# A decoder layer on one core: the order of its first 40 microseconds rebuilt

## The chip, the cores and the metric

The kernel runs on one core of one Trainium2 chip. The core has five engines that run beside each other, each with its own queue, taken strictly in order: TensorE (PE; its weight loads are listed as PEld), VectorE (DVE), ScalarE (ACT), GpSimd (POOL) and SyncE (SP), which here only issues DMA transfers. Engines wait for each other by semaphores. The metric is the device time of one execution in microseconds (us); lower is better.

## The reference

One layer of a decoder trunk over 256 positions of width 2048, all in fp32:

```python
mod = silu(c) @ w_ada + b_ada                      # 6 segments of 2048
shift1, scale1, gate1, shift2, scale2, gate2 = split(mod, 6)
h = rms_norm(x, norm1_gain) * (1 + scale1) + shift1
x = x + gate1 * mixing_sublayer(h, w_in, ...)      # h @ w_in, three attention branches, output projection
h = rms_norm(x, norm2_gain) * (1 + scale2) + shift2
x = x + gate2 * swiglu(h, w_ffn_in, w_ffn_out)
```

with `rms_norm(x, g) = x * rsqrt(mean(x*x) + eps) * g`. For the beginning only the first three lines matter: nothing of `h @ w_in` can start before the norm of x, and before shift1 and scale1, each of which is a product of silu(c) with a 2048 x 2048 part of `w_ada`. Later parts (attention, gated linear attention, branch gates, output projection, feed-forward) are the same before and after.

## The kernel before, in words

**Products in three matmuls.** A product keeps fp32 accuracy by splitting both operands: `hi` is the value rounded to the matmul's format (fp32r), `lo` what is left. `mm3` (L151 to L154) adds hi x hi, hi x lo and lo x hi into one PSUM bank. A weight piece is loaded by SP into one of four `raw` buffers (L135), cast to `whi` on ScalarE (L146) and subtracted to `wlo` on VectorE (L147); then `raw` is free again.

**Blocks and groups.** `h @ w_in` is computed in column blocks of 512 (13 blocks, `proj_block`), for both halves of the 256 positions. The 16 tiles of 128 along the width are taken in four groups, `GROUPS` = 0 to 3, 3 to 7, 7 to 11, 11 to 16. A group's 13 blocks need only that group's h, so the first blocks can start when shift1 and scale1 are known for three tiles. A block of the first group has 3 tiles x 2 halves x 3 matmuls = 18 matmuls. Results go to `A[b]` by copies on ScalarE (L415).

**Shift and scale.** `ada_group` computes them without TensorE's big products: SP loads a piece of `w_ada` for each of 16 tiles k (L269; for the first group 128 x 768: three tiles of shift and of scale), and VectorE multiplies it by silu(c) of that tile and adds it to `acc` (`ada_mac`, L247 and L249). At the end `column_sum` (L292) sums over the partitions by a matmul with ones; `finish_columns` (L298, L301) adds b_ada and applies norm1_gain. The next group's pieces are loaded and added while a group's blocks run.

**The norm of x.** `norm1` loads x in four pieces of 128 x 1024 (L344), sums squares on ScalarE (L355), combines them on VectorE (L356, L358), and takes 1/sqrt by `rsqrt`: Ln and Exp on ScalarE (L232, L233) and one Newton step on VectorE (L230, L235 to L238). ScalarE scales x in place (L362), TensorE turns it in 32 transposes (L366), ScalarE copies the result to `xT` (L367). `make_h` (L376 to L378) makes h from it: hi and an fp32 copy on ScalarE, lo on VectorE.

**Vectors.** `load_vectors` brings gains and biases as rows (three loads on SP, L207 to L209, seven on POOL, L216 to L219) and turns them into columns with two transposes (L221, L224). c has its own load and transpose (L190, L192) and becomes `csil` = silu(c).

**What sets the order.** A planner orders each engine's queue ahead of time: among instructions that its own estimate of time holds ready, it takes the one of highest priority. `prio` raises the priority of what is written inside it; otherwise what is written earlier goes first. `tc.issue_after(i)` puts the instructions inside it behind instruction i, when they are on i's engine. Tiles named by a tag (`S(tag, ...)`) share one place in memory; a new tile of the tag waits until the old one is read for the last time. `scr` is a pool of three such places. In the old beginning, four pieces of `w_ada` are issued (`XAT`), then the norm and the vectors, then the other pieces; the junk output of the squares, c, and the two tiles of vector rows all take `scr` places.

Of the kernel before, what the change touches and what calls it, by code (L numbers as in the profile page):

```python
# [34 lines left out]
XAT = 4  # L35
AHEAD = 4000
FIN = 13
# [28 lines left out]
def trunk(ctx: ExitStack, tc: tile.TileContext, I, out):  # L66
# [57 lines left out]
    def load_weights(src, k0, k1, c0, w=NB, spare=()):  # L124

        parts = []
        step = (2 * NB) // w  # L130
        with prio():
            for ka in range(k0, k1, step):
                n = min(step, k1 - ka)
                raw = wp.tile([P, step, w], F32, tag="raw", name=nm("raw"))
                nc.sync.dma_start(  # L135
                    raw[:, :n, :],
                    src[ka * P : (ka + n) * P, c0 : c0 + w].rearrange("(k p) c -> p k c", p=P),
                )
# [7 lines left out]
                nc.scalar.copy(hi[:, :n, :], raw[:, :n, :])  # L146
                state["split"] = nc.vector.tensor_tensor(lo[:, :n, :], raw[:, :n, :], hi[:, :n, :].bitcast(F32), op=ALU.subtract)  # L147
                parts += [(hi[:, i, :], lo[:, i, :]) for i in range(n)]
        return parts
# [27 lines left out]
    make_identity(nc, ident)  # L177
    ones = const.tile([P, P], F32, name="ones")
    nc.vector.memset(ones, 1.0)
    ones_r = const.tile([P, P], F32R, name="ones_r")  # L180
    nc.scalar.copy(ones_r, ones)
# [10 lines left out]
    nc.tensor.transpose(c_ps, crow[:KC, :], ident[:KC, :KC])  # L192
# [8 lines left out]
    rows = scr([P, P])  # L201
    brow = scr([P, P])
# [3 lines left out]
    def load_vectors():  # L206
# [3 lines left out]
        for r, name in (  # L210
            (ROW_SBQ, "sb_q_gain"),
            (ROW_SBK, "sb_k_gain"),
            (ROW_DILQ, "dil_q_gain"),
            (ROW_DILK, "dil_k_gain"),
        ):
            nc.gpsimd.dma_start(rows[r : r + 1, :], I[name])  # L216
        nc.gpsimd.dma_start(rows[ROW_GB : ROW_GB + 4, :], by_chunk("b_gla_a"))
        nc.gpsimd.dma_start(rows[ROW_GG : ROW_GG + 2, :], by_chunk("gla_out_gain"))
        nc.gpsimd.dma_start(rows[0:16, :], by_chunk("c"))  # L219
# [4 lines left out]
        nc.tensor.transpose(bada_ps, brow[:96, :], ident[:96, :96])  # L224
# [66 lines left out]
    def column_sum(ps, acc):  # L291
        nc.tensor.matmul(ps, acc, ones[:, 0:1], start=True, stop=True)  # L292
# [47 lines left out]
    def norm1():  # L340
        xin = [S(f"A{9 + j}", [P, 2, NB]) for j in range(4)]
        for t in range(NT):
            for hf in range(2):
# [3 lines left out]
                )  # L347
        for t in range(NT):
            ss2 = small([P, 2])
            for hf in range(2):  # L350
                junk = scr([P, 512])
                xs = xin[2 * t + hf]
                pa = small([P, 2])
                for q in range(2):
                    nc.scalar.activation(junk, xs[:, q, :], AF.Square, accum_out=pa[:, q : q + 1])  # L355
                nc.vector.tensor_add(ss2[:, hf : hf + 1], pa[:, 0:1], pa[:, 1:2])  # L356
            ss = small([P, 1])
            nc.vector.tensor_add(ss, ss2[:, 0:1], ss2[:, 1:2])  # L358
            rstd = rsqrt(ss, 1.0 / D, [P, 1])
            for hf in range(2):  # L360
                xs = xin[2 * t + hf]
                nc.scalar.activation(xs, xs, AF.Copy, scale=rstd)  # L362
                for q in range(2):
                    ps = misc_bank([P, 4, P])
                    for i in range(4):
                        nc.tensor.transpose(ps[:, i, :], xs[:, q, i * P : (i + 1) * P], ident)  # L366
                    nc.scalar.copy(xT[2 * hf + q][:, :, t * P : (t + 1) * P], ps)  # L367
# [3 lines left out]
    def make_h(k, sh, sc):  # L371
# [4 lines left out]
        nc.scalar.activation(hi, src, AF.Identity, bias=sh, scale=sc)  # L376
        nc.scalar.activation(hf, src, AF.Identity, bias=sh, scale=sc)
# [43 lines left out]
    def h_group(g):  # L421
        k0, k1 = GROUPS[g]
        sh, sc = gains[g]
        for k in range(k0, k1):
            make_h(k, sh[:, k - k0 : k - k0 + 1], sc[:, k - k0 : k - k0 + 1])

    with prio(30000):
        early = []
        g0 = ada_group(
            *GROUPS[0],  # L430
            tags=tuple(f"A{j}" for j in range(9)) + ADA_TAGS,
            between=lambda: early.extend(load_weights(w_in, *GROUPS[0], orders[0][0] * NB)),
        )
        for _ in range(XAT):
            next(g0)
        with prio():
            norm1()
            load_vectors()
        for _ in g0:
            pass  # L440
        with prio():
            h_group(0)
    qg_sb = const.tile([P, 2], F32, name="qgains")
# [4 lines left out]
    for g in range(len(GROUPS) - 1):  # L448
# [636 lines left out]
```

## Time and profile before

| | |
|---|---|
| median of 3 executions | 1640.3 us (1639.02 to 1644.5) |
| the profiled execution | 1639.62 us, of which the span is 1637.8 us |
| TensorE busy | 1599.9 us (98%), 7309 matmuls |
| VectorE, ScalarE busy | 1120.5 us, 801.8 us |
| first matmul of the first block | 34.63 us after the start of the span |
| first matmul of the second block | 40.66 us |

The span runs from the first to the last instruction of the profiled execution; times within it are counted from its start. A row of the order of time gives start, length, engine, line, operation, what is written from what, a count of merged instructions, and in brackets how long the engine was idle before and what ended that. The length of matmuls is modelled and overlaps; the distance of their starts is what they cost. The row PEclk is the share of TensorE's full clock that was granted. A plain fp32 matmul stands as two records, a transpose as one.

### The profile page before, as it was taken

How to read it: one execution, taken by the hardware profiler on the slowest of the kernel's cores; microseconds unless marked ns; L12 is line 12 of the kernel's file. 1: busy time of each engine (PE TensorE's matmuls, PEld its weight loads, DVE VectorE, ACT ScalarE, POOL GpSimd, SP SyncE). 2: the span in 40 equal slices, each digit the busy share in tenths (PEclk: the TensorE clock that was granted, in tenths of full speed). 3: DMA queues.
4: the chain of work that ended last, by engine and by line, in shares of the span. 5: the costliest groups of instructions: out<-in, count | busy, mean ns of one | idle time of the engine just before them, and what ended most of it. 6: DMA issues, size and time to landing. Idle time of an engine off the chain costs nothing.

```text
span 1637.8 us, 19950 instructions
## 1 busy us (share of the span) xinstructions
PE 1599.9 (98%) x7309; PEld 1320.3 (81%) x7309; DVE 1120.5 (68%) x1351; ACT 801.8 (49%) x1133; POOL 6.0 (0%) x14
## 2 busy tenths in 40 slices
PE   4999999999999999999999999999999999999998
PEld 3788888788778888888887888888888888888887
DVE  6789996879687687877756566766655555454453
ACT  5654448765765444444445644444444444433332
POOL 1000000000000000000000000000000000000000
PEclk9999999999999999999999999999999999999999
DMA  9999987776777899888757478888766666666663
GB/s 316 322 327 323 325 285 216 250 242 186 225 229 263 295 312 310 305 270 311 260 184 226 131 231 260 280 260 255 222 189 192 181 192 189 187 207 195 206 206 109
DMA packets 194562, 395.91 MB, mean 242 GB/s; under 512 B 12899, under 2 KB 27913, under 8 KB 194465
## 3 DMA queue, kind: packets, MB, share of 16 engines
q1 hardware_dynamic: 194240, 394.63, 74.7%
q8 instruction: 57, 0.93, 0.2%
q14 instruction: 41, 0.33, 0.1%
q0 software_dynamic: 224, 0.01, 0.0%
HBM read 392.50 MB, written 2.10 MB: 241 GB/s over the span
## 4 chain that ended last, share of the span: by engine, by line
PE 91%; DVE 3%; DMA 2%; ACT 2%; issue 1%; SPq 0%; DVEq 0%; ACTq 0%
PE acc L153 28%; PE acc L154 28%; PE acc L152 28%; DVE wlo L147 1%; DMA raw<-w_br_gla 1%; PE misc L606 1%; PE misc L871 1%; PE misc L292 1%; ACT whi L146 1%; DVE ada L249 1%; PE misc L366 0%; DMA A<-x 0%; PE misc L500 0%; DMA AR<-w_ada 0%; DMA raw<-w_ffn_in 0%
## 5 line engine op out<-in xcount | busy, mean ns | idle before, releaser
L147 DVE TENSOR_TENSOR wlo<-raw,whi 128x1024 fp32r<-128x1024 f32 (+1 forms) x548 | 653.4, 1198 | 435.9 <-ACT whi L146 432.6
L146 ACT CAST whi<-raw 128x1024 fp32r<-128x1024 f32 (+1 forms) x548 | 564.2, 1032 | 706.1 <-PE acc L154 556.5
L153 PE MATMUL acc<-wlo,H 128*128 128x512 f32 x1576 | 617.5, 392 | 3.1 <-DVE wlo L147 3.0
L152 PE MATMUL acc<-whi,H 128*128 128x512 f32 x1576 | 615.6, 392 | 2.2 <-ACT whi L146 2.1
L154 PE MATMUL acc<-whi,H 128*128 128x512 f32 x1576 | 616.0, 391 | 0.0
L153 PEld LDWEIGHTS acc<-wlo,H 128*128 128x128 f32 x1576 | 296.3, 188 | 67.0 <-DVE wlo L147 7.8
L152 PEld LDWEIGHTS acc<-whi,H 128*128 128x128 f32 x1576 | 296.0, 188 | 63.4 <-ACT whi L146 3.0
L154 PEld LDWEIGHTS acc<-whi,H 128*128 128x128 f32 x1576 | 296.3, 188 | 62.2 <-DVE H L378 0.9
L152 PE MATMUL acc<-whi,A 128*128 128x512 f32 x312 | 122.3, 392 | 0.0
L153 PE MATMUL acc<-wlo,A 128*128 128x512 f32 x312 | 121.5, 390 | 0.7 <-DVE wlo L147 0.7
L154 PE MATMUL acc<-whi,A 128*128 128x512 f32 x280 | 109.1, 390 | 0.0
L249 DVE SCALAR_TENSOR_TENSOR ada<-AR,csil,ada 128x1024 f32<-128x1024 f32 x59 | 75.1, 1278 | 1.6 <-DMA AR<-w_ada 1.5
L153 PEld LDWEIGHTS acc<-wlo,A 128*128 128x128 f32 x312 | 58.6, 188 | 13.0 <-DVE wlo L147 1.1
L152 PEld LDWEIGHTS acc<-whi,A 128*128 128x128 f32 x312 | 58.6, 188 | 12.0
L154 PEld LDWEIGHTS acc<-whi,A 128*128 128x128 f32 x280 | 52.5, 188 | 11.1
L152 PE MATMUL acc<-whi,T 128*128 128x512 f32 x120 | 46.8, 390 | 0.0
L154 PE MATMUL acc<-whi,T 128*128 128x512 f32 x120 | 46.7, 389 | 0.0
L153 PE MATMUL acc<-wlo,T 128*128 128x512 f32 x120 | 46.7, 389 | 0.0
L154 PE MATMUL acc<-whi,OS 128*128 128x512 f32 x112 | 43.6, 389 | 0.0
L415 ACT COPY A<-acc 128x512 f32<-128x512 f32 x50 | 28.6, 586 | 21.1 <-PE acc L154 20.1
L249 DVE SCALAR_TENSOR_TENSOR ada<-OS,csil,ada 128x1024 f32<-128x1024 f32 (+2 forms) x33 | 35.5, 1075 | 0.5 <-DMA OS<-w_ada 0.2
L417 DVE TENSOR_TENSOR A<-A,acc 128x512 f32<-128x512 f32 x48 | 31.9, 684 | 5.1 <-PE acc L154 4.9
(315 smaller groups left out, 1217.3 us busy)
## 6 DMA issues: line engine op xcount, KB each, us to landing
raw<-w_in SPq DMA_DIRECT2D x205, 512.0 KB, 4.7
raw<-w_ffn_in SPq DMA_DIRECT2D x176, 512.0 KB, 4.1
raw<-w_ffn_out SPq DMA_DIRECT2D x88, 512.0 KB, 4.8
AR<-w_ada SPq DMA_DIRECT2D x79, 512.0 KB, 4.9
raw<-w_out SPq DMA_DIRECT2D x32, 512.0 KB, 4.3
KC<-w_ada SPq DMA_DIRECT2D x30, 512.0 KB, 5.0
KD<-w_ada SPq DMA_DIRECT2D x19, 512.0 KB, 5.8
OS<-w_ada SPq DMA_DIRECT2D x16, 512.0 KB, 6.6
```

The costliest lines, as they stand in the source:

```text
L146: nc.scalar.copy(hi[:, :n, :], raw[:, :n, :])
L147: state["split"] = nc.vector.tensor_tensor(lo[:, :n, :], raw[:, :n, :], hi[:, :n, :].bitcast(F32), op=ALU.subtract)
L152: nc.tensor.matmul(ps, lh, rh, start=start, stop=False, skip_group_check=seeded)
L153: nc.tensor.matmul(ps, lh, rl, start=False, stop=False, skip_group_check=seeded)
L154: state["mm"] = nc.tensor.matmul(ps, ll, rh, start=False, stop=stop, skip_group_check=seeded)
L249: nc.vector.scalar_tensor_tensor(acc, raw, c, acc, op0=ALU.mult, op1=ALU.add)
L292: nc.tensor.matmul(ps, acc, ones[:, 0:1], start=True, stop=True)
L415: nc.scalar.copy(A[b][:, t, :], pss[t])
L417: nc.vector.tensor_add(A[b][:, t, :], A[b][:, t, :], pss[t])
L606: nc.tensor.matmul(ps[:, h, :], at(lhs, h, t), at(rhs, h, t), start=True, stop=True)
L871: nc.tensor.transpose(ps[:, i, :], src[:, i * P : (i + 1) * P], ident)
```

## The change

The order of the beginning is new. SP issues c, the vectors, x, and then all 16 pieces of the first group's `w_ada`, followed by the first block's `w_in`. c, the vector rows, the squares' junk, the diagonal and an operand for unused matmuls get places that belong to h later (H2, H3, H5 to H7, H0 and H1), none in `scr`. POOL's loads are put right behind the making of the identity matrix.

The norm's sums, the Newton step and the reciprocal root run on ScalarE alone, for both halves of the positions together. x is not scaled any more: TensorE multiplies each 128 x 128 tile of x by a diagonal matrix of the reciprocal roots, which turns and scales it at once. So 32 transposes become 32 plain fp32 matmuls.

Between the steps TensorE gets matmuls whose result nobody reads (`keep_warm`, 128 x 512, fp32r): 22 behind the transpose of c, 20 behind the transposes of the vectors, 32 behind the turning of x, 5 behind the column sums. The turning of the vectors is put behind the first 22, and the column sums behind the 32. The six column sums of the first group go to one PSUM tile, and all of them are issued before the first is finished.

The first block's casts on ScalarE are put behind the last copy to `xT`, and h of the first group behind these casts. The casts of later weights, up to the sixth block, are put behind the first instruction of h. In the first group the fp32 copy of h is made on VectorE. `ones_r` is made on VectorE instead of ScalarE.

```diff
-XAT = 4
+WARM = (22, 20, 32, 5)
@@ load_weights(..., ahead=True)
-                nc.scalar.copy(hi[:, :n, :], raw[:, :n, :])
+                with tc.issue_after(state["casts_after"]) if "casts_after" in state else nullcontext():
+                    state["cast"] = nc.scalar.copy(hi[:, :n, :], raw[:, :n, :])
@@
-    crow = scr([P, P])
+    crow = S("H7", [P, P])
-    rows = scr([P, P])
-    brow = scr([P, P])
+    rows = S("H6", [P, P])
+    brow = S("H5", [P, P])
@@ load_vectors: the seven POOL loads
+        with tc.issue_after(made):
...
+    def turn_vectors():
...
@@ norm1
+        for t in range(NT):
             for hf in range(2):
-                junk = scr([P, 512])
...
+                junk = S(f"H{t}", [P, 2, NB])
+                act(junk, xin[2 * t + hf], AF.Square, accum_out=part[:, hf, t : t + 1])
+        v, y, z, r = (small([P, NT]) for _ in range(4))
+        col = lambda a, t: a[:, t : t + 1]
+        for t in range(NT):
+            act(col(v, t), part[:, 0, t : t + 1], AF.Identity, bias=part[:, 1, t : t + 1])
+        act(v, v, AF.Identity, bias=eps_c[:, 0:1], scale=1.0 / D)
+        act(y, v, AF.Ln)
+        act(y, y, AF.Exp, scale=-0.5)
+        act(z, y, AF.Square)
+        for t in range(NT):
+            act(col(z, t), col(z, t), AF.Copy, scale=col(v, t))
+        act(z, z, AF.Identity, bias=eps_c[:, 1:2], scale=-0.5)
+        diag = S("H3", [P, NT, P])
+        for t in range(NT):
+            act(col(r, t), col(y, t), AF.Copy, scale=col(z, t))
+            act(diag[:, t, :], ident, AF.Copy, scale=col(r, t))
+        for j in range(4):
+            for t in range(NT):
+                ps = misc_bank([P, 4, P])
+                for i in range(4):
+                    xs = xin[2 * t + j // 2][:, j % 2, i * P : (i + 1) * P]
+                    state["turn"] = nc.tensor.matmul(ps[:, i, :], xs, diag[:, t, :], start=True, stop=True)
+                state["turned"] = nc.scalar.copy(xT[j][:, :, t * P : (t + 1) * P], ps)
+
+    def keep_warm(n):
+        ps = acc_bank()
+        for _ in range(n):
+            state["warm"] = nc.tensor.matmul(ps, ones_r, wide, start=True, stop=True)
+
+    wide = S("H2", [P, NB], F32R)
@@ make_h(k, sh, sc, early=False)
-        nc.scalar.activation(hf, src, AF.Identity, bias=sh, scale=sc)
+        if early:
+            nc.vector.tensor_scalar(hf, src, sc, sh, op0=ALU.mult, op1=ALU.add)
+        else:
+            nc.scalar.activation(hf, src, AF.Identity, bias=sh, scale=sc)
@@
+    def first_group():
...
+            nc.sync.dma_start(r, w_ada[k * P : (k + 1) * P, : 2 * D].rearrange("p (s c) -> p s c", s=2)[:, :, :w])
+            raws.append(r)
+        with tc.issue_after(state["turned"].ins):
+            early.extend(load_weights(w_in, *GROUPS[0], orders[0][0] * NB, ahead=False))
+        last_cast = state["cast"]
+        acc = S("ada", [P, 2, w])
+        for k in range(KC):
+            ada_mac(acc, raws[k], k)
+        ps = misc_bank([P, 2 * n])
+        for q in range(n):
+            for j in range(2):
+                with tc.issue_after(state["warm"].ins):
+                    last_sum = column_sum(ps[:, 2 * q + j : 2 * q + j + 1], acc[:, j, q * P : (q + 1) * P])
+        with tc.issue_after(last_sum.ins):
+            keep_warm(WARM[3])
...
     with prio(30000):
...
+        load_vectors()
+        load_x()
+        with tc.issue_after(c_turn.ins):
+            keep_warm(WARM[0])
+        with tc.issue_after(state["warm"].ins):
+            turn_vectors()
+        with tc.issue_after(state["row_turn"].ins):
+            keep_warm(WARM[1])
+        norm1()
+        with tc.issue_after(state["turn"].ins):
+            keep_warm(WARM[2])
+        last_cast = first_group()
+        with prio(), tc.issue_after(last_cast.ins):
             h_group(0)
+        state["casts_after"] = state["h_first"].ins
@@ the loop over blocks
+            if (g, n) == (0, 6):
+                state.pop("casts_after", None)
```

More of the change, by code (lines that the diff above doesn't have):

```diff
@@ L357, in norm1 @@
[L357 to L367, printed above, removed]
+                junk = S(f"H{t}", [P, 2, NB])
@@ L424, in h_group @@
         for k in range(k0, k1):
-            make_h(k, sh[:, k - k0 : k - k0 + 1], sc[:, k - k0 : k - k0 + 1])
-    with prio(30000):
[L428 to L441, printed above, removed]
+            make_h(k, sh[:, k - k0 : k - k0 + 1], sc[:, k - k0 : k - k0 + 1], g == 0)
```

71 lines of the change are left out of this document (45 added, 26 removed).

## The prediction

> **What bounds the kernel now.** I read the page first, then a table of stages, then the instructions in order of time.
>
> ```profile
> span 1637.8 us, 19950 instructions
> PE 1599.9 (98%) x7309; PEld 1320.3 (81%) x7309; DVE 1120.5 (68%) x1351; ACT 801.8 (49%) x1133; POOL 6.0 (0%) x14
> ...
> PE   4999999999999999999999999999999999999998
> ...
> PEclk9999999999999999999999999999999999999999
> DMA  9999987776777899888757478888766666666663
> ```
>
> TensorE is the bound: 37.9 us of the span are not PE, and nearly all of them lie in the first slice (41 us). A change of the beginning can win what lies there and little more. The table of stages cuts that slice and the steady part behind it:
>
> ```profile
> 16.10:20.00 3.90, 3.68 (x16) 3.28 (x16) 3.28 (x5) 3.83 (x10) 0.93 (x2) 1.00 0.78 235
> 20.00:24.10 4.10, 0.00 (x0) 0.00 (x0) 3.26 (x10) 2.65 (x7) 0.00 (x0) 1.00 0.96 305
> 24.10:27.70 3.60, 3.53 (x16) 3.28 (x16) 3.28 (x4) 2.81 (x5) 0.00 (x0) 1.00 1.05 381
> 27.70:31.10 3.40, 0.73 (x5) 0.46 (x4) 2.75 (x5) 0.84 (x3) 0.00 (x0) 1.00 1.05 388
> 31.10:34.60 3.50, 2.38 (x12) 2.29 (x12) 0.97 (x9) 1.55 (x3) 0.00 (x0) 0.50 1.05 387
> 34.60:37.90 3.30, 3.23 (x7) 1.88 (x8) 3.29 (x6) 3.30 (x7) 0.00 (x0) 0.50 0.73 209
> 54.00:87.00 33.00, 32.47 (x143) 26.58 (x143) 26.74 (x26) 20.62 (x31) 0.00 (x0) 1.00 0.94 333
> ```
>
> Each row: the stage, its length, busy time of PE, PEld, DVE, ACT and POOL, then granted clock, DMA share and GB/s. The clock is half from 31.1 to 37.9, just when the sums and the first block run. Before 27.7 the column says 1.00 only because no change was recorded yet: the transposes there (L366) take 421 ns, those at full clock later (L500) 273 ns, so it was half. DMA falls to 235 GB/s in 16.1 to 20.0. The order of time shows the path:
>
> ```profile
> 10.30 0.63 ACT L355 ACTIVATE scr<-A 128x512 f32<-128x512 f32 x1 [7.43 <-DMA A<-x]
> ...
> 29.78 1.02 DVE L249 SCALAR_TENSOR_TENSOR ada<-A,csil,ada 128x768 f32<-128x768 f32 x1
> ...
> 30.95 2.53 PE L292 MATMUL misc<-ones,ada 128*128 128x1 f32 x12 [2.67 <-DVE ada L249]
> 31.88 0.22 DVE L298 TENSOR_TENSOR mod<-misc,bada 128x1 f32<-128x1 f32 x2 [1.07 <-PE misc L292]
> ...
> 33.05 0.60 ACT L376 ACTIVATE H<-T,mod 128x256 fp32r<-128x256 f32 x1 [4.33 <-DVE mod L301]
> 33.55 1.55 ACT L146 CAST whi<-raw 128x1024 fp32r<-128x1024 f32 x2
> ...
> 34.63 1.22 PE L152 MATMUL acc<-whi,H 128*128 128x512 f32 x2 [1.16 <-ACT whi L146]
> ```
>
> The first block waits for h; h for the column sums; those for the last of 16 multiply-adds (macs) on VectorE. The second block's first matmul starts at 40.66. A block has 18 matmuls, each 0.227 us after the one before at full clock (starts 42.70, 42.93, 43.16), that is 4.09 us; so the first block cost as if it had run undisturbed from 36.57. That is the figure to beat. Last, what SP waits for in the first 100 us:
>
> ```profile
> SPq L135 <- DVE wlo L147: 41.9, 21, 5.2
> SPq L135 <- DMA raw<-w_in: 5.0, 4, 1.9
> ```
>
> Weight loads wait for a free raw buffer, not for DMA. Bandwidth is no bound once blocks run.
>
> **Vectors and x first.** SP issues c, three vectors (0.33, 0.33, 0.42 us) and four pieces of x (0.60 each) before the 16 pieces of w_ada (0.47 each): x begins at about 2.2 instead of 3.18, w_ada at 4.6 instead of 1.19. POOL's seven issues (0.5 each, 3.6 together) ran from 13.45, after a 12.1 us wait for a shared scratch buffer; they now follow the identity matrix at 1.3 and, at 4.1 to 5.5 us to landing, are there by 9.5. SP's waits for the same buffers (1.6 and 4.2 us), where DMA dipped, go. The same 2.1 + 6.3 MB come as one stream: between 351 GB/s (stage 2.4 to 16.1) and 388, from about 3.4, the last w_ada lands between 25.0 and 27.4, and its mac (1.02) ends at about 27.5, at most 28.5. The two w_in pieces (0.79 MB, 2 us) land at about 28.5.
>
> **The norm on ScalarE.** VectorE loses 16 tiny operations (about 0.155 each, 2.5 us) and their waits, so the macs (1.02 against one piece per 1.0 to 1.1 us of DMA) keep pace with the stream. ScalarE loses four scalings of x (1.14 each) and has 4 squares of 1024 columns instead of 8 of 512 (0.75 each with the read of the sum): about 1.2 each. The last x lands at about 9.7, the last square ends at 10.9. Then 13 small operations in a row, 0.24 apart (Ln to Exp, 13.75 to 13.99); those with a per-partition operand cost more: L376 with two takes 586 ns for 256 columns, the plain copy L415 takes 586 for 512, so 0.1 us each. Eleven operations with eight operands, 3.5 us: first diagonal at 14.4, second at 15.0. VectorE gains the fill of the unused matmuls' operand (between 0.17, the memset at L179, and 0.68, a 512-column subtract) and three copies of h (between 0.2, a quarter of L247's 0.745, and 0.42, L378); both lie where it is idle.
>
> **Transposes become matmuls by a diagonal.** A plain fp32 matmul stands as two records (L520: 12 for 6 heads), 0.113 apart at full clock (L606: 16 in 1.8 us). So 32 cost 64 x 0.113 = 7.2 us where 32 old transposes at half clock cost 7.36. At half clock they would cost 14.7. ScalarE's eight copies (0.59 against 0.9 per group) stay hidden.
>
> **The unused matmuls set the beat.** All are written into TensorE's order, so the start of the first block is now a sum on one queue: c turned at 2.65; 22 matmuls, 0.43 apart at half clock (L152 x2: 1.22 less the 0.79 of one). The records change at 27.7, 31.1 and 37.9, on a grid of 3.4 us; work from 24.17 had full clock after 3.5, from 34.63 after 3.3, and 3.7 us of work from 16.19 never (the next transposes still take 421 ns). So full clock comes 3.4 to 6.8 us after the start, I take 5.1: 12 slow, 10 fast, end 10.05 (9.25 to 10.85). The Trainium skill, "TensorE: Matmul & The Clock Gate", Part 1, puts the release at about 4 us into sustained work, with 0.5 either way; by it the 22 would end at 9.5 and the total be 1634.6 (an estimate). Two of the three stretches agree with it, the third does not.
>
> Vectors turned, 0.5: 10.55. 20 matmuls, 4.54: 15.1 (diagonals are there by then, with no slack for the second). Turns 7.2: 22.3. 32 matmuls, 7.26: 29.6; the macs are done, and the column sums, placed behind these matmuls, start here. Sums 12 x 0.106 (1.68 for 16 at 87.07) = 1.27, half of the 2.53 of before: 30.9. All six sums now share one PSUM tile, so I let the finishing wait for the last: three operations and h end at about 32.0. Five matmuls, 1.14: 32.0. Handover 0.1: the first block starts at **32.1** and ends at 36.2. Behind the waits stand, in order, all that TensorE does later; nothing else of it is late.
>
> **Casts.** The first block's casts (1.03 + 0.61) now run ahead of h, in ScalarE's idle time; with splits (1.22 + 0.68) they are done at about 31.0. So its matmuls need not wait as they did at 34.63, 35.89 and 36.91. Later casts stand behind the first h at 31.5; block 1's is needed at 36.2 and takes 1.7: hidden, unless h slips by over 3 us.
>
> **Sum.** 40.66 - 36.2 = 4.4 us earlier, at unchanged work behind. The profiled execution took 1639.62 (span 1637.8 and 1.8 around it), 0.7 under the median 1640.3: 1635.2. From the median that is 0.31%, and 0.3%, about what a measurement of this kernel can tell, is 1635.4. Bounds of the unknown terms: the clock's phase 0.8 either way, handovers and stalls in block 0 from 0 to 1.5: 1634.2 to 1637.5.
>
> **Rivals.**
> *A later stall goes too.* At 52.45 to 53.98 TensorE waits through a cast and its split, because on ScalarE the cast stands behind a copy of a finished block. Other order of casts could dissolve it: 1.4 less, 1633.8. Against: blocks after the seventh are ordered as ever.
>
> *The head start is eaten.* Transfers from 54 to 87 run at 333 GB/s of the 388 seen; if blocks that begin 4.4 us sooner meet the same landing times, TensorE idles as much more: 1639.6. Against: SP's 41.9 us of waits are for buffers, which come free sooner too.
>
> *The chain of the norm outlasts its cover.* No slack at 15.1: each us that x or an operand is late is a us lost; at 1.5 us, 1636.7. Over 3.4 us the clock falls too, as in 27.7 to 31.1.
>
> *The first block's splits stand ahead of macs on VectorE* (slower). The early load is now written before the macs and at the same priority, and VectorE takes its queue in order. If the planner thinks w_in lands before the last w_ada, n macs follow splits that end at 31.0: the sums start at 31.1 + 1.03 n instead of 29.6. With n = 5 (the macs not yet landed when xT is ready, 22.9) that is 36.2, +6.6: 1641.8. From n = 3 it is slower than before, from n = 9 (1646.0) by over 0.3%. For it: nothing orders splits behind macs. Against: in this trace L147 first runs at 34.61, behind all macs.
>
> **Chances.** Forecast 0.49 (0.27 under 1635.4, 0.22 over); later stall 0.18, faster; eaten 0.07 and chain 0.04, both within; splits 0.22 (0.06 within, 0.16 slower). Faster 0.45, within 0.39, slower 0.16. The range runs to 1632.8 below (stall gone and full clock early) and 1643.5 above (splits with n up to 6); about 0.2 lies outside, most of it above. The forecast's own range is 1633.5 to 1637.5.
>
> **What would show it.** First block's L152 at 31.3 to 33 and the second block's 4.1 us later; clock full from before 10 us on; no gap between the macs; L147 behind the last mac; sums at the end of the unused matmuls, not waiting for VectorE. Wrong if TensorE waits for the diagonal or for a mac, if L147 precedes an L249 of the first group, or if idle time of PE between 40 and 200 grows by over 1 us.

## The result, and the profile after

The changed kernel takes 1637.31 us in the median of 20 runs (1635.15 to 1639.23), the kernel before 1642.25 us in 20 runs beside it. The ratio is 0.9969, with a 95% interval of 0.9962 to 0.9976: 4.9 us or 0.31% faster. The profiled execution took 1638.33 us (span 1636.6).

The first view of the changed kernel is the page: the span, the busy times, and the busy share of DMA in 40 slices (41 us each).

```profile
span 1636.6 us, 20156 instructions
...
PE 1617.2 (99%) x7420; PEld 1333.7 (81%) x7420; DVE 1120.2 (68%) x1342; ACT 798.2 (49%) x1126; POOL 5.9 (0%) x14
...
DMA  9999986876778889888756478887766666666663
```

TensorE is busy for 17.3 us more, but the 79 unused matmuls alone take 21.8 us of the first slice, so the busy share says nothing about the gain. DMA is as busy as before. The span fell by 1.2 us only, less than the runs: the profiled execution of the kernel before took less time than most of its executions (1639.62; the mean of all 95 executions of it is 1642.2). We come back to this.

The order of time of the changed kernel shows how the beginning runs now (start, length, engine, line, operation; in brackets the idle time and what ended it).

```profile
10.40 1.06 ACT L366 ACTIVATE H<-A 128x1024 f32<-128x1024 f32 x1 [2.40 <-DMA A<-x]
...
12.50 1.04 ACT L366 ACTIVATE H<-A 128x1024 f32<-128x1024 f32 x1
...
16.98 7.41 PE L389 MATMUL misc<-H,A 128*128 128x128 f32 x64 [1.16 <-ACT H L383]
...
24.14 7.70 PE L396 MATMUL acc<-H,ones_r 128*128 128x512 f32 x32
...
29.56 1.02 DVE L258 SCALAR_TENSOR_TENSOR ada<-A,csil,ada 128x768 f32<-128x768 f32 x1
30.83 1.57 ACT L147 CAST whi<-raw 128x1024 fp32r<-128x1024 f32 x2 [5.82 <-DMA raw<-w_in]
...
31.68 1.39 PE L301 MATMUL misc<-ones,ada 128*128 128x1 f32 x12
31.91 1.83 DVE L148 TENSOR_TENSOR wlo<-raw,whi 128x1024 fp32r<-128x1024 f32 x2 [1.32 <-ACT whi L147]
...
33.65 0.35 DVE L307 TENSOR_TENSOR mod<-misc,bada 128x1 f32<-128x1 f32 x4
...
34.16 1.09 ACT L408 ACTIVATE H<-T,mod 128x256 fp32r<-128x256 f32 x2 [1.77 <-DVE mod L307]
...
34.81 0.50 PE L153 MATMUL acc<-whi,H 128*128 128x512 f32 x1 [0.48 <-ACT H L408]
```

Three things are to be seen. The first block starts at 34.81, no sooner than before (34.63). What precedes it is no longer TensorE's own order: the last multiply-add ends at 30.58, `w_in` is cast from 30.83, the splits follow on VectorE until about 33.7, and only then the modulation is finished (L307), so that h and the block can begin. And the first block, once started, meets no stall: the second block's first matmul runs at 39.03, that is 4.22 us later, where the kernel before needed 6.03 (34.63 to 40.66). So the start brought nothing and the block itself 1.8 us.

The table of stages says why. It cuts the changed kernel where its own work changes: stage, length, busy time of PE, PEld, DVE, ACT and POOL, granted clock, DMA share, GB/s.

```profile
0.00:10.50 10.50, 7.96 (x23) 6.05 (x23) 1.46 (x8) 2.71 (x5) 4.26 (x13) 1.00 0.66 207
10.50:16.90 6.40, 5.20 (x23) 3.89 (x22) 3.04 (x6) 6.17 (x21) 0.00 (x0) 1.00 1.06 381
...
24.10:31.70 7.60, 7.60 (x36) 6.16 (x35) 6.03 (x6) 1.48 (x3) 0.00 (x0) 1.00 1.05 380
31.70:34.80 3.10, 2.64 (x18) 2.08 (x16) 2.89 (x12) 1.33 (x4) 0.00 (x0) 1.00 1.05 387
34.80:39.00 4.20, 4.18 (x18) 3.43 (x19) 4.10 (x10) 2.52 (x4) 0.00 (x0) 1.00 0.97 359
```

The clock is full in the stages of the sums and the first block, where it was half before. DMA runs without a dip from 10.5 to 34.8 (373 to 387 GB/s). But the first 10.5 us move 207 GB/s only. In steps of 5 us, the same table of the kernel before begins with 156 and 329 GB/s and dips to 266 later; the changed kernel's begins with 59 and 337:

```profile
0.00:5.00 5.00, 0.26 (x1) 0.18 (x1) 0.76 (x4) 1.77 (x3) 0.70 (x6) 1.00 0.54 156
5.00:10.00 5.00, 0.00 (x0) 0.00 (x0) 2.66 (x3) 0.00 (x0) 0.00 (x0) 1.00 1.03 329
...
15.00:20.00 5.00, 3.68 (x16) 3.28 (x16) 4.15 (x5) 4.93 (x10) 2.03 (x5) 1.00 0.84 266
```

```profile
0.00:5.00 5.00, 2.46 (x6) 2.00 (x7) 1.46 (x8) 1.47 (x2) 4.26 (x13) 1.00 0.28 59
5.00:10.00 5.00, 5.00 (x17) 3.94 (x16) 0.00 (x0) 1.15 (x2) 0.00 (x0) 1.00 1.00 337
...
15.00:20.00 5.00, 3.84 (x31) 3.36 (x30) 4.28 (x7) 3.33 (x13) 0.00 (x0) 1.00 1.06 372
```

Summed over the six steps up to 30 us, the kernel before moves 9.27 MB and the changed one 9.53 MB: 0.26 MB more, 0.7 us of transfer at 386 GB/s. The last piece of `w_ada` gets nothing of this. In the trace it lands at 29.46, and in the kernel before at 29.26. The transfers run side by side: when that piece lands, 0.79 MB of pieces issued behind it are already there, 0.48 MB in the kernel before. The last multiply-add nevertheless ends 0.2 us sooner than before (30.58 against 30.80), because VectorE is no longer behind: it begins 0.1 us after the landing (29.56) instead of 0.5 us (29.78).

For the rest of the kernel we follow one number, the **lead**: by how much the same ScalarE and VectorE instructions run sooner than in the first profile of the kernel before (median over a stretch). In the changed kernel it is 1.4 us at 48 us and 2.4 to 2.8 from 60 to 300 us. So a further 1.0 to 1.4 us comes in between. PE's idle time from 40 to 200 us falls from 2.01 to 0.88 us. The place is the hand-over from the fourth block to the fifth. First the kernel before, then the changed one, in the order of time:

```profile
52.42 0.59 ACT L415 COPY A<-acc 128x512 f32<-128x512 f32 x1 [2.81 <-PE acc L154]
52.90 1.05 ACT L146 CAST whi<-raw 128x1024 fp32r<-128x1024 f32 x1
...
54.00 0.73 PE L152 MATMUL acc<-whi,H 128*128 128x512 f32 x2 [0.94 <-ACT whi L146]
...
55.27 0.50 PE L153 MATMUL acc<-wlo,H 128*128 128x512 f32 x1 [0.53 <-DVE wlo L147]
```

```profile
50.09 1.05 ACT L147 CAST whi<-raw 128x1024 fp32r<-128x1024 f32 x1 [1.87 <-DMA raw<-w_in]
51.05 1.25 ACT L451 COPY A<-acc 128x512 f32<-128x512 f32 x2
...
52.46 0.50 PE L154 MATMUL acc<-wlo,H 128*128 128x512 f32 x1 [0.33 <-DVE wlo L148]
```

Before, ScalarE's queue has a copy of the fourth block's result ahead of the fifth block's cast. ScalarE waits 2.81 us for that block to end, although the fifth block's weights have landed by 51.56, and TensorE then waits 0.94 and 0.53. In the changed kernel the cast stands ahead of both copies, and 0.33 us of waiting is left. Nothing in the diff names this order: the planner chose it anew. Why it did is not shown.

### The profile page after: what moved, and what is told of

It is laid out like the page before. It is cut to its first block, busy times and chain, and to the rows that moved or that the text cites. A ratio compares the mean times of both kernels' runs of the same rounds, so it can differ in the third digit from the quotient of the medians.

```text
span 1636.6 us, 20156 instructions
## 1 busy us (share of the span) xinstructions
PE 1617.2 (99%) x7420; PEld 1333.7 (81%) x7420; DVE 1120.2 (68%) x1342; ACT 798.2 (49%) x1126; POOL 5.9 (0%) x14
## 4 chain that ended last, share of the span: by engine, by line
PE 90%; DMA 4%; DVE 3%; ACT 2%; issue 1%; SPq 0%; DVEq 0%; ACTq 0%
PE acc L154 28%; PE acc L155 28%; PE acc L153 28%; DMA raw<-w_in 2%; DVE wlo L148 1%; DMA A<-w_ada 1%; PE misc L678 1%; ACT whi L147 1%; PE misc L943 1%; PE misc L301 1%; DVE ada L258 1%; DMA raw<-w_br_gla 0%; PE misc L572 0%; DMA AR<-w_ada 0%; DMA raw<-w_ffn_in 0%
## 5 line engine op out<-in xcount | busy, mean ns | idle before, releaser
L148 DVE TENSOR_TENSOR wlo<-raw,whi 128x1024 fp32r<-128x1024 f32 (+1 forms) x548 | 653.6, 1197 | 436.4 <-ACT whi L147 432.9
```

## The experiments

All kernels here compute the full result. The order of the table is that of the text; the lead is in us, and a kernel's time is the median of its runs.

```
kernel                 lead at 48   at 84   at 700   at the end   time      ratio [95% interval]
changed                  1.39       2.43    1.09       1.28       1637.31   0.9969 [0.9962, 0.9976]
a1 changed, again        1.51       3.04   -0.20       0.42       1637.55   0.9975 [0.9966, 0.9983]
a2 no unused matmuls     0.54       0.54    1.93       2.51       1639.54   0.9987 [0.9978, 0.9995]
a3 26 instead of 32      1.62       3.24    1.15       1.53       1637.35   0.9969 [0.9957, 0.9980]
a4 unused alone          0.57       0.58   -0.25       0.39       1639.85   0.9987 [0.9978, 0.9995]
b1 before, again        -0.89      -0.88   -2.29      -1.85       1641.46   (one run)
b2 x, then vectors       1.98       3.35    2.46       2.88       1637.30   0.9974 [0.9964, 0.9983]
b3 finish first          1.87       1.87    3.28       3.74       1637.74   0.9978 [0.9968, 0.9988]
b4 b2 and b3             2.53       2.56    1.27       1.77       1636.74   0.9967 [0.9954, 0.9980]
c1 before, cast first   -2.83      -1.08   -1.32      -1.20       1640.84   0.9991 [0.9981, 1.0000]
c3 changed, copy first   1.41       1.41    0.44       0.53       1638.31   0.9977 [0.9968, 0.9986]
c2 b4, cast first        2.48       3.74    1.86       2.47       1636.00   0.9967 [0.9954, 0.9979]
d1 c2, again             2.31       4.35    4.19       4.41       1636.89   0.9962 [0.9948, 0.9976]
```

**a1: the changed kernel once more.** No edit.

> The changed kernel once more, unaltered, for a second profile. In the first pair of profiles the second block's first matmul came at 39.03 instead of 40.66, 1.6 us sooner, and by 60 us the lead was 2.8; after that the lead fell by 2.0 at about 335 us and by 0.9 at about 688 us (TensorE waited for late weights) and grew by 1.7 at 488 us, where only the old kernel's clock fell to half for 3.4 us. Theory A (what comes after 60 us is chance of the single execution): second block again at 39.0 (38.6 to 39.6), and the two losses not at the same places. Theory B (the change causes the later losses): idle time of TensorE again at about 330 and 688. Time in both: ratio to before 0.996 to 0.998.

First block at 34.69, first copy of its result at 38.88, last multiply-add at 30.44: within 0.2 us of the first profile. The lead at 84 us is 3.04. Up to there the two executions agree. Then a1 loses 1.1 us between 88 and 100 us, where its clock is half from 87.23 to 90.64; the first profile has the full clock there. The table of stages of a1 has this row:

```profile
87.30:90.60 3.30, 3.23 (x8) 2.56 (x9) 2.13 (x5) 3.30 (x7) 0.00 (x0) 0.50 0.65 187
```

By 700 us a1 has lost 3.2 us, the first profile 1.3. The two waits that the theories ask about come at the same matmuls in both profiles, but differ in length: 2.88 us at 334.22 in the first, 1.13 at 333.68 in a1, and 0.71 and 1.18 near 687 us. The kernel before waits at these matmuls too (0.90 and 0.54). So the places are fixed, as theory B has it, but the change did not make them, and how long the wait is falls by execution.

**a2: no unused matmuls.** Nothing else is edited, but the planner orders VectorE and ScalarE otherwise here: the finishing of the sums goes ahead of the splits, and the fifth block's cast behind a copy again, as in the kernel before.

```diff
-WARM = (22, 20, 32, 5)
+WARM = (0, 0, 0, 0)
 def keep_warm(n):
+    if n == 0:
+        state.setdefault("warm", c_turn)
+        return
```

> All four groups of unused matmuls left out, everything else of the change kept. Theory clock: the matmuls that turn x start at half clock and warm it up, then TensorE idles from about 27 until the last multiply-add ends at 30.6, so the clock falls again in most executions; sums and first block run at half clock; second block at 40.5 to 42, 1.5 to 3 us slower than the changed kernel. Rival loads: the start is set by the transfers, the casts and VectorE, and the clock costs nothing there; second block at 39 to 39.5, time within 0.5 us of the changed kernel.

The order of time of this kernel, and then its row of stages for the first block:

```profile
31.54 0.35 DVE L307 TENSOR_TENSOR mod<-misc,bada 128x1 f32<-128x1 f32 x4 [1.72 <-PE misc L301]
...
32.71 1.22 PE L153 MATMUL acc<-whi,H 128*128 128x512 f32 x2 [1.28 <-ACT H L411]
...
33.42 1.22 DVE L148 TENSOR_TENSOR wlo<-raw,whi 128x1024 fp32r<-128x1024 f32 x1
...
34.70 0.79 PE L154 MATMUL acc<-wlo,H 128*128 128x512 f32 x1 [0.78 <-DVE wlo L148]
```

```profile
31.20:37.90 6.70, 4.65 (x13) 3.21 (x13) 6.26 (x19) 2.72 (x5) 0.00 (x0) 0.52 0.94 323
```

The first block starts 2.1 us sooner than in the changed kernel, because here the finishing (L307) stands ahead of the splits (L148). Yet its result is copied at 39.63, 0.6 us later than the changed kernel's: the clock is half (0.52) and the matmuls wait for the splits. The ratio 0.9987 is about half of the changed kernel's gain or less. The second block's first matmul comes at 40.12, between what the two theories expected. The time is 2.0 us over the changed kernel's, but not all of that is the clock, since the cast behind the copy costs 1.0 to 1.6 us of it (c3 below).

**a3: 26 instead of 32 unused matmuls behind the turns.**

```diff
-WARM = (22, 20, 32, 5)
+WARM = (22, 20, 26, 5)
```

> 26 instead of 32 unused matmuls before the column sums, all queues else in the same order. The sums could start 1.36 us sooner, at 30.7 when the last multiply-add ends. Theory VectorE: the finishing of the sums stands behind the two splits of the first weights (31.91 to 33.74), so h and the first block stay at 34.2 and 34.8: no gain, at most 0.2. Rival TensorE's written order: the first block comes at 33.4, the time falls by 1.4.

```profile
30.49 1.47 PE L301 MATMUL misc<-ones,ada 128*128 128x1 f32 x12
...
31.63 1.83 DVE L148 TENSOR_TENSOR wlo<-raw,whi 128x1024 fp32r<-128x1024 f32 x2 [1.29 <-ACT whi L147]
...
33.38 0.35 DVE L307 TENSOR_TENSOR mod<-misc,bada 128x1 f32<-128x1 f32 x4
...
34.54 0.50 PE L153 MATMUL acc<-whi,H 128*128 128x512 f32 x1 [1.31 <-ACT H L408]
```

The column sums start 1.2 us sooner (30.49 against 31.68), the first block only 0.27, and the time is the same. So the number of unused matmuls does not set the start. The splits stand between the sums and their finishing on VectorE, and they wait for casts that wait for `w_in`.

**a4: the unused matmuls alone, in the kernel before.** 18 behind the first transposes of x, 16 behind the turned vectors, 5 behind the column sums; nothing else is changed.

```diff
+WARM = (18, 16, 5)
...
+            if t == 0:
+                with tc.issue_after(state["turn"].ins):
+                    keep_warm(WARM[0])
...
+            with tc.issue_after(state["row_turn"].ins):
+                keep_warm(WARM[1])
...
+                    if k0 == 0 and q == m - 1:
+                        with tc.issue_after(last_sum.ins):
+                            keep_warm(WARM[2])
```

> The kernel before with nothing but unused matmuls added: 18 after the first 16 transposes, 16 after the transposes of the vectors, 5 after the column sums. Theory clock: sums take 1.3 instead of 2.5 and the first block runs at full clock, second block at 39.2 to 39.8 instead of 40.66, and the time falls by 1 to 2.5 us, most of what the whole change wins at the start. Rival order of loads: the last multiply-add ends at 30.8 as before and the casts still stand behind h, so the second block stays at 40.3 to 40.7 and the time within 0.5.

The row of stages shows the clock full where it was 0.50:

```profile
31.20:37.90 6.70, 5.55 (x27) 3.77 (x27) 4.50 (x16) 4.93 (x9) 0.00 (x0) 1.00 1.00 354
```

The first block starts at 34.56 and its result is copied at 39.58 instead of 40.18, though the last multiply-add ended 0.6 us later here (31.38 against 30.80). The ratio is 0.9987. The second block's first matmul comes at 40.06, again between the two theories. The clock without the new order gives as much as the new order without the clock, 0.13% each; the two together give 0.25 to 0.31%, in which the later stall (below) has a part that neither a2 nor a4 has.

**b1: the kernel before once more.** No edit.

> The kernel before once more, unaltered, for a second profile of it. Theory phase: the clock changes on a grid of 3.4 us, and in the first profile the first block met it early (full clock 3.3 us after the block began, the least there can be); in another execution the half clock reaches up to 3.4 us further into the block, and the second block starts at 40.7 to 42.4. Rival: the grid is tied to the start of the program, the second block starts at 40.66 again and the clock rises at 38.0.

The last multiply-add ends at 31.70 and the first block starts at 35.40, 0.8 us after the first profile. The bytes moved by 30 us are 8.80 MB instead of 9.27. The beginning of c1 is that of the kernel before as well, and there the first block starts at 36.49 (8.82 MB). The block took 6.15 us (35.40 to 41.55) against 6.03, with the full clock 3.60 us after its start against 3.33. So the second block starts where the theory of the clock's phase had it, but 0.8 of the 0.9 us were lost ahead of the block, with the late multiply-adds. The profile that the prediction started from was the best of three. In the kernels with the changed kernel's beginning the start is steady: 34.81, 34.69 and 34.77 (changed, a1, c3).

**b2: x ahead of the vectors.**

```diff
-        load_vectors()
-        load_x()
+        load_x()
+        load_vectors()
```

> The changed kernel with one edit on one queue: SP issues the three vector loads after the four pieces of x instead of before them; all other queues are the same instruction by instruction. Theory transfers: x and all loads behind it come 1.2 us sooner (three issues of 0.41 each), so the first diagonal is ready at 15.7 instead of 16.9, the first w_in piece lands at 29.6 instead of 30.8, the first block starts at 33.6 and the time falls by 1.0 to 1.3 us against the changed kernel. Rival ramp: the slow beginning of the transfers (under 300 GB/s until 6 us) is no matter of issue, x lands when it did, and the time stays within 0.4.

```profile
8.97 1.06 ACT L366 ACTIVATE H<-A 128x1024 f32<-128x1024 f32 x1 [2.49 <-DMA A<-x]
...
30.22 1.57 ACT L147 CAST whi<-raw 128x1024 fp32r<-128x1024 f32 x2 [5.82 <-DMA raw<-w_in]
...
34.21 0.50 PE L153 MATMUL acc<-whi,H 128*128 128x512 f32 x1 [0.47 <-ACT H L408]
```

x is issued 1.39 us sooner (1.19 against 2.58) and its squares start 1.4 to 1.5 us sooner, but the second still starts 3.6 us after the first, as in the changed kernel, and the last piece lands 1.1 us sooner (10.52 against 11.63). The last `w_ada`, the casts and the first block come 0.6 us sooner, half of what the theory of transfers expected, and the lead at 84 us is 3.35. In the time that doesn't show (0.9974 against 0.9969 and 0.9975). The three small issues ahead of x cost 0.6 us; the rest of what comes late is, as far as the rows show, the slow beginning of the transfers and the pieces that share the stream.

**b3: the finishing ahead of the splits.** The early load is written behind the finishing, with its casts and splits ordered after the first finished column; h's fp32 copy is made on ScalarE again, and 26 unused matmuls stand behind the turns.

```diff
-        with tc.issue_after(state["turned"].ins):
-            early.extend(load_weights(w_in, *GROUPS[0], orders[0][0] * NB, ahead=False))
...
+        with tc.issue_after(state["turned"].ins), tc.issue_after(finished.ins):
+            early.extend(load_weights(w_in, *GROUPS[0], orders[0][0] * NB, ahead=False))
```

> The changed kernel with the splits of the first weights put behind the finishing of the first pair of sums on VectorE, the fp32 copy of the first h made on ScalarE as in the kernel before, and 26 instead of 32 unused matmuls before the sums. Theory VectorE: the first h starts at 32.3 instead of 34.2, the first lo matmul (which needs a split) at 33.6 to 34.0 instead of 35.15, and the time falls by 1.0 to 1.5 us against the changed kernel. Rival: what is won at the first block is waited for at the second, whose weights come no sooner; time within 0.4.

In the order of time of this kernel the finishing is now first, and the block starts a microsecond sooner (its result is copied at 37.76 against 39.01):

```profile
32.64 0.35 DVE L307 TENSOR_TENSOR mod<-misc,bada 128x1 f32<-128x1 f32 x4 [1.72 <-ACT whi L147]
...
33.18 1.21 DVE L148 TENSOR_TENSOR wlo<-raw,whi 128x1024 fp32r<-128x1024 f32 x1
...
33.81 0.73 PE L153 MATMUL acc<-whi,H 128*128 128x512 f32 x2
...
52.13 0.73 PE L153 MATMUL acc<-whi,H 128*128 128x512 f32 x2 [0.94 <-ACT whi L147]
```

The time is not better than the changed kernel's. The last line says why: the stall of 0.94 us behind the cast is back, and the lead stays at 1.87 where a1's grows to 3.04. The planner had put the copy ahead of the cast again.

**b4: b2 and b3 together** (20 unused matmuls in the second group become 18).

> The last two edits together (x ahead of the vectors; finishing ahead of the splits; 22, 18, 26 and 5 unused matmuls). Theory: the two gains add, the first block starts at 31.5 to 32.5 and the time falls by 2.0 to 2.8 us against the changed kernel, ratio to before 0.995 to 0.996. Rival: the weights of the first blocks come no sooner than they did, so the sum is no more than the larger of the two.

First block at 33.10, its result at 38.03, and a lead of 2.53 that stays 2.56, again with the stall. The lead at 48 us is more than that of b2 (1.98) or b3 (1.87), but the first block comes later than expected (31.5 to 32.5), and the time of 1636.74, 0.6 us under the changed kernel's, is not clear of noise.

**c1 and c3: the order of cast and copies alone.** c1 is the kernel before, with the copies of the fourth block's result written behind the fifth block's casts. VectorE's and SP's queues stay the same; on TensorE one matmul of each of two later blocks moves, from 59 us on.

```diff
+            if (g, n) == (0, 4):
+                early[:] = load_weights(w_in, *GROUPS[0], b * NB)
+                with prio(), tc.issue_after(state["first_cast"].ins):
+                    ...
+                    for t in range(NT):
+                        nc.scalar.copy(A[b3][:, t, :], late[t])
```

c3 is the changed kernel with the old order put back at this place (some instructions further on, from 53 us, change places with it: two splits on VectorE, a cast on ScalarE, and one matmul of each of two later blocks).

```diff
+            if (g, n) == (0, 4):
+                state["casts_after"] = state["copies"][0].ins
+            if (g, n) == (0, 5):
+                state.pop("casts_after", None)
```

> The kernel before, with one thing moved: on ScalarE's queue the two copies of the fourth block's accumulators (COPY A<-acc at 49.6 and 52.4 us of the profile of before) stand behind the fifth block's two casts instead of the first of them standing in front. Nothing else is reordered: VectorE's and SyncE's queues are the same. Theory 'the later stall is a matter of this order': the stall of 1.4 us at 52 to 54 us (matmul 0.94 on whi, 0.53 on wlo) goes, the first matmul of the fifth block waits at most 0.4, and the second block of copies behind it comes 1.0 to 1.4 sooner than in the kernel before of the same start; time 1.0 to 1.4 us less, ratio 0.9991 to 0.9994. Rival 'the stall goes only when the blocks start sooner or at the full clock': the cast then waits for something else (its transfer), the stall stays above 1 us, and the ratio is 1.000 within 0.0005.

> The changed kernel with one thing put back: the fifth block's first cast stands behind the first of the fourth block's copies on ScalarE's queue, as in the kernel before (the fourth and third queues are the same, VectorE's but for one swap). Theory 'the later stall is a matter of this order': the lead of 1.4 to 1.5 at 48 us stays 1.4 to 1.5 at 60 us instead of 2.8; time 1.0 to 1.4 us more than the changed kernel, ratio 0.9978 to 0.9984. Rival 'the changed kernel loses the stall because its blocks run at the full clock from the start': the lead at 60 us is 2.4 or more all the same, and the ratio 0.9969 to 0.9975.

c3 in the order of time:

```profile
51.02 0.59 ACT L452 COPY A<-acc 128x512 f32<-128x512 f32 x1 [2.81 <-PE acc L155]
...
52.60 0.73 PE L153 MATMUL acc<-whi,H 128*128 128x512 f32 x2 [0.94 <-ACT whi L147]
```

The stall is back to the hundredth (2.81, 0.94), and the lead stays at 1.41. The time is 1.0 us over the changed kernel's and 0.8 over a1's, with 0.9977 against 0.9969 and 0.9975. These intervals overlap, so the times alone do not show it; the rows and the lead do. In c1 the fifth block's casts run ahead of the copies:

```profile
53.94 1.57 ACT L146 CAST whi<-raw 128x1024 fp32r<-128x1024 f32 x2 [1.50 <-DVE ada L250]
...
55.42 1.10 ACT L466 COPY A<-acc 128x512 f32<-128x512 f32 x2
```

Its first matmul on `wlo` follows at 56.31, 0.3 us late. This execution began late (first block at 36.49), so its lead is -2.83 at 48 us. It is -1.08 from 60 us on: 1.8 us came back at this hand-over, although neither the start nor the clock of the first block was better than before. So the stall is a matter of this order. The ratio 0.9991 lies where it was expected, though its interval reaches 1.0.

**c2 and d1: b4 with the cast ahead of the copies,** the same edit as in c1.

> The kernel b4_both (x issued ahead of the vectors, finishing of the modulation ahead of the splits, 26 unused matmuls, lead of 2.5 us at 48 us) with the same reordering as c1. Theory 'two separate gains that add': the lead of 2.5 at 48 us becomes 3.7 to 4.0 at 60 us, the time 1.0 to 1.4 under b4_both, 1635.3 to 1636.2, ratio 0.9960 to 0.9965 (where the places past 300 us that change by execution give it back, up to 0.9970). Rival 'a lead of that size runs into the transfers of w_in': the lead falls back to about 2.5 to 3 by 84 us with matmuls waiting on casts that wait for raw<-w_in, ratio as b4_both, 0.9967.

> The kernel c2_both_cast_first once more, for its time and for a second profile of where its lead of 3.7 us at 84 us goes. Theory 'what is lost past 300 us falls by chance of the execution': lead again 3.5 to 3.9 at 84 us, the losses at other places or of other size than in c2 (there 0.3 at 312, 0.4 at 336 and 1.3 between 400 and 480 us), time 1634.8 to 1636.8, ratio 0.9957 to 0.9972. Rival 'a kernel that is further ahead runs into the same wait each time': the losses at the same three places and of the same size within 0.2.

Both gains are there: the lead goes from 2.3 to 2.5 at 48 us to 3.74 and 4.35 at 84 us. In d1 it is more than the 3.5 to 3.9 expected. c2 loses 1.9 of its 3.7 us by 700 us, d1 0.2 of its 4.4, so the theory of chance holds against the same wait each time: the waits are at the same places, but not of the same size. The two differ most at one place near 485 us, where TensorE waits for VectorE. In the order of time, first the kernel before, then c2, then d1:

```profile
488.14 0.71 PE L715 MATMUL misc<-ident,T 128*128 128x128 f32 x3 [2.37 <-DVE T L711]
```

```profile
486.39 0.61 PE L801 MATMUL misc<-ident,T 128*128 128x128 f32 x3 [3.71 <-DVE T L797]
```

```profile
484.35 0.61 PE L801 MATMUL misc<-ident,T 128*128 128x128 f32 x3 [2.53 <-DVE T L797]
```

The same program waits 1.2 us longer in c2 than in d1. And the clock behind it differs, as the table of stages shows (c2, then d1):

```profile
484.00:494.00 10.00, 7.61 (x37) 6.57 (x38) 5.24 (x18) 3.14 (x6) 0.00 (x0) 0.83 0.85 295
```

```profile
484.00:494.00 10.00, 9.63 (x58) 7.94 (x59) 5.09 (x17) 5.14 (x10) 0.00 (x0) 1.00 0.86 305
```

Before and c2 have the half clock in a part of this stage, d1 and the changed kernel do not; these gain lead there over the first profile of before (the changed kernel 0.81 to 2.28 by 495 us, of which 1.85 are left at 500; d1 3.7 to 5.28, of which 4.45 are left).

The ten runs of the two take 1636.5 us in the mean, the 31 of the changed kernel (with a1) 1637.5: 1.0 us less. By their ratios (0.9967 and 0.9962, intervals about 0.0013 either way) the advantage over the changed kernel is likely but not shown.

## Why the prediction was right, and where it was not

The forecast was 1635.2 us, 4.4 us under the profiled execution of before. The time is 2.1 us over that forecast and within the range; the medians differ by 4.9 us, faster by 0.31%. That lies at the 0.3% from which the prediction speaks of faster: with an interval of 0.24% to 0.38%, and 0.25% in a1, its outcomes faster and within are hardly told apart. That the difference is near the 4.4 us of the forecast is luck. The head start was a third of that, and two things filled the gap: a gain that had been left to a rival, and a profile of before that was better than most.

**TensorE's order sets the beat: wrong.** This is the step that failed. The head start at the second block is 1.63 us (40.66 to 39.03), not 4.4. Its terms in turn:

- x last landed at 9.7 by the sum, and in the trace at 11.63. The last two squares stand behind each other on ScalarE at 11.46 and 12.50, so the last one ends at 13.6, not 10.9. The sum had moved the transfers forward by the issue times, at 351 to 388 GB/s from 3.4 on; the first 5 us move 59 GB/s.
- The last `w_ada` was to land between 25.0 and 27.4 and its multiply-add to end by 28.5. They came at 29.46 and 30.58. To the slow beginning comes that the sum had each piece land before the next one moved. The 0.79 MB of later pieces that are there by then are 2.1 us at 380 GB/s (an estimate from the stage 24.1 to 31.7).
- The chain of 13 small operations was priced at 3.5 us and took 3.5 (13.5 to 17.0). It began late, so the turns waited 1.16 us for the diagonal, one of the prediction's own signs of being wrong. The rival of the norm chain was right on the mechanism but could not decide, as a3 shows: TensorE had time to spare behind it.
- The 32 turns took 7.2 us (16.98 to 24.14), as priced, the sums 1.26 (1.27).
- `w_in` was to land at 28.5 and the splits to end at 31.0. The cast waited for the transfer until 30.83, and the splits ended at about 33.7. So the casts did run ahead of h, but 2.7 us later than forecast.
- The finishing was let wait for the last sum only. It also stood behind the splits on VectorE, and h could not start before 34.16 (forecast by 32.0). So the rival of VectorE's queue was near: the splits did not precede the multiply-adds, but they did precede the finishing. b3 puts that at about 1 us.
- Three smaller slips change nothing of this. Of the 37.9 us that are not PE, 24.1 lie in the first 41 us, not nearly all. From 1635.2 the clock's 0.8 leads down to 1634.4, not to 1634.2, and the last lines give 1633.5 for the same bound. And in 27.7 to 31.1, the example for idle time of over 3.4 us, TensorE idles for 2.67 us.

**Clock: right.** The clock was full from 8.09, 5.36 us after the unused matmuls began (forecast 5.1 of 3.4 to 6.8). In a1, a3, b2, b3, b4, c2, c3 and d1 it took 6.1, 3.3, 5.6, 4.8, 4.0, 3.4, 6.1 and 5.6 us. The Trainium skill, "TensorE: Matmul & The Clock Gate", Part 1, would have 4 us with 0.5 either way; of these nine only b4 lies inside. Of the three stretches that the prediction set beside it (3.5, 3.3, never) only the first does, not two. Nothing hung on it, since TensorE waited later anyhow. The first block ran in 4.22 us against 6.03, close to the undisturbed 4.09. The other executions agree: the granted clock over the span (what lies ahead of the first recorded change counts as full) is 0.9950 in the mean of 75 executions of the kernel before and 0.9987 in 31 of the changed kernel. The clock alone (a4) and the new order alone (a2) bring 0.13% each.

**The later stall: the rival came true.** It had a chance of 0.18 and a price of 1.4 us. c1 and c3 measured 1.8 and 1.0 to 1.6 us. The reason given against it, that blocks after the seventh are ordered as ever, does not bear on the stall, which stands at the fifth. The ordering of the casts behind h does not bring the better order by itself: a2, b3 and b4 have it too, and there the copy stands ahead of the cast. Which part of the change does is not shown.

**The base.** The forecast was counted from 1639.62, and the mean of the kernel before is 1642.2. Three profiles of its beginning (before, b1, c1) have the first block at 34.63, 35.40 and 36.49, and leads at 48 us of 0, -0.89 and -2.83, -1.2 in the mean. The lead of the changed kernel at 84 us, 2.4 and 3.0 in two profiles, added to that gives 3.9 us. The measured differences are 4.9 and, in a1's comparison, 4.3. So the terms are 1.4 to 1.6 of head start, 1.0 to 1.5 of the stall, and 1.2 from a beginning that no longer comes late: 3.6 to 4.3 of the 4.3 to 4.9. The last term rests on three executions only.

What stays open is where leads change behind 84 us. By 700 us they fell by 1.3 and 3.2 us in the two profiles of the changed kernel and by 1.4 in b1, and grew by 1.4 in a2 and b3. A part of that is the clock, which is half for 3.41 us near 87 us in a1 and b2 (1.1 us lost), from 685.24 in a3 (1.5 lost), and near 490 us in others: it is there in before, b1, a4, b2, b4, c2 and c3, and not in the changed kernel, a1, a2, a3, b3, c1 and d1, so it does not go with a part of the change. For the rest, no run fixes the cause: in the changed kernel 2.0 us is lost near 334 us, where TensorE waits 2.88 us for a split, and in a1 0.2 us, where it waits 1.13.

## What to carry to other kernels

Price a reordering of the beginning from the bytes that have landed by then, not from the times at which they are issued: here the new order of transfers moved 0.26 MB more by 30 us, none of it for the last piece of `w_ada`, whatever TensorE's own queue allowed. Behind an edit, compare the instruction order of every queue also where nothing was edited; a copy that slipped ahead of a cast was worth as much as the head start. And take a second profile of the kernel before, since a forecast counted from a lucky execution is too low from the first line.

## What the runs showed of the hardware

The first transfers are slow: 59 GB/s in the first 5 us with x issued from 2.58 (156 in the kernel before, whose first piece of `w_ada` is issued at 1.19). In both the changed kernel and b2 the second 512-KB piece of x is used 3.6 us after the first, with x issued at 2.58 or at 1.19. A later stream ran at 372 to 387 GB/s.

The clock can fall for a short stretch in the middle of the kernel, in some executions and not in others of the same program: behind a wait of 3.71 us near 485 us it fell in c2, behind one of 2.53 us in d1 it did not, yet behind one of 2.37 us it fell in the kernel before and behind one of 3.13 us in a1 it did not. So the length of the wait does not decide. In a1 it fell at 87.23, although TensorE is listed as busy for 3.19 of the 3.40 us ahead (16 column sums among them). Such a stretch cost 0.8 to 1.5 us. The time until the full clock at the start varied from 3.3 to 6.1 us among kernels that begin alike, and in c2 and d1 the clock fell once more for 3.41 us, from 12.90 and from 32.06; in d1 that is in the first block.
